# A hybrid mixer layer on one core: where the output weights are split, how many rooms the sample attention has, and in which round one product stands

## The chip, the cores and the metric

The kernel runs on one core of a Trainium2 chip. The metric is the device time of one execution in microseconds (us), the median of the runs. One more execution was taken by the profiler; all rows below come from it.

The engines are named as in the profile: PE (TensorE's matmuls; PEld its weight loads), DVE (VectorE), ACT (ScalarE), POOL (GpSimd) and SP (SyncE, which issues DMAs). SPq is SP's own queue.

## The reference, cut to what matters

One mixer layer is computed for a prompt of 1024 tokens and for 8 samples of 8 tokens (64 rows), 1088 rows in all, with the same weights. Three branches (retention, multi-scale pooling, sparse attention) are merged by sigmoid gates and go through one output projection.

```python
z = rms_norm(x, gain) @ w_in
o_a, s_ret_new = retention(rq, rk, rv, s_ret, pos0)          # 4 heads
b_a = (silu(rg) * o_a) @ w_br_a
o_b, pool_new = pool_mix(pu, pool_buf, pos0, w_pool, pool_scale)
b_b = (silu(pg) * o_b) @ w_br_b
o_c = nsa_attention(nq, kv_cmp, kv_sel, kv_win, ...)
b_c = (silu(ng) * o_c) @ w_br_c
merged = gates[0] * b_a + gates[1] * b_b + gates[2] * b_c
y = x + merged @ w_out                                        # w_out: 1024 x 1024
y = rms_norm(y, final_gain)
```

## The kernel before, in words

**Numbers in two halves.** A float32 operand is held as two float16 tiles, high and low part, and a product is three matmuls (high by high, low by high, high by low). `wsplit` (L220 to L224) makes the two parts of a weight: a scaled copy on ACT (L222), then a subtraction on DVE (L223).

**Stages.** `run` (L161) goes through the stages in order: keys and values of the prompt, prompt attention, retention (about 495 to 760 us of the profiled execution), the sample stage (760 to 887 us: the pooling branch and `sample_attention`), and `output` (from 887 us: the branch products and the merge by Strassen's scheme, and from 1212.6 us `out_rows`, the product with w_out).

**Retention.** 36 steps, 4 heads by 9 tiles of rows. Each step projects one tile (`proj_t`, 24 matmuls into a tile z) and moves the tiles in flight one stage on (`ret_tile`, a generator: rotation, rh, a transposing DMA qt, scores at and am, ah and al, output ro, state S and Sh). `load_r` fetches and splits the next head's weights (rwh, rwl) at the head's third tile. From the seventh step on, each step also calls the generator `sample_prep` once, which prepares the samples' compressed keys.

**Sample stage.** PE does the projections of the pooling branch (pj, L309 to L311, three matmuls of 384 or 320 columns per block) and between them `sample_attention`. That runs over four pairs of samples: keys and values into ks and vs, scores s, softmax in s and st (S and sums), transposes ta (L1089) and tb (L1091), their float16 parts sph (ACT, L1096) and spl (DVE, L1097), products so (L1108, L1111), their sum soc, and a transpose sto (L1117). The tiles svs, sks, sS and sst have one room each, so that a pair takes the room of the pair before it. Last in the stage's code, `out_weights` (L1504) fetches w_out in 8 blocks of 512 KB (tile wr), splits each (wh on ACT, wl on DVE, 128x1024) and stores both parts in DRAM (wod, two stores of 256 KB a block) for the output stage to read back.

**Output.** `out_rows` multiplies the merged rows (mm) by w_out in blocks of 128 rows by 512 columns; with Strassen's sums T1 to T4 of quarters of w_out, which are made beside it: DVE subtracts quarters (L1800) and `wsplit` splits the sums into tb, rm and T4a. A `prod` is 12 matmuls of 512 columns (L1841), a `plus` adds its result on DVE (L1846). The first round (four row blocks) does two products a block, then `remainder` does the last 64 rows, and the second round does five products a block: S2 by T2, S1 by T1, S4 by the plain quarter 22, S3 by T3, and 22 by T4. Behind them a block is finished: a square on ACT (L1849), a sum and a power (DVE L1854 and L416, POOL L417), and two multiplications on DVE (L1862, in the function `finish`), then the store. POOL adds the intermediate sums (L1915, L1922, L1925).

**What sets the order.** The code is recorded, and a scheduler then gives each engine one fixed list of instructions, by its own estimate of when each would be ready. A tile's number of rooms (`bufs`) and the pools bound how far it can interleave. Under `with self.behind()` the instructions are placed behind the marked ones of the main work. An engine takes its list in order.

## Time and profile before

| what | us |
|---|---|
| median of the runs | 1308.41 |
| the runs | 1307.53, 1308.41, 1314.39 |
| the profiled execution's own time | 1306.29 |
| its span | 1304.5 |
| PE busy in the span | 1251.3 (96%) |
| DVE busy | 912.2 (70%) |
| ACT busy | 631.3 (48%) |
| POOL busy | 525.2 (40%) |

The span is the time from the first to the last instruction that the profiler saw; the execution's own time is 1.8 us more, and the median of the runs another 2.1 us more. In the rows a matmul's duration contains its fill; the pitch of two matmuls is the difference of their starts. "Idle before" in square brackets is the time in which the engine had nothing to do just before an instruction, with what ended it.

### The profile page before, as it was taken

To read this page: it belongs to the slowest core of one execution; us is meant where nothing else is said; L and a number is where in the kernel's file an instruction comes from. 1 tells how busy PE (TensorE), PEld (TensorE's weight loads), DVE (VectorE), ACT (ScalarE), POOL (GpSimd) and SP (SyncE) were. 2 spreads that over 40 slices of the span, in tenths; PEclk is the share of its full clock that TensorE was granted. 3 is DMA by queue.
4 is the path that set the end of the run, shared out by engine and by line. 5 is a ranking of instruction groups with operands and counts; after the bars stand their busy time and mean duration, and the time that the engine had idled before them with its cause. 6 is when DMAs were issued, how large, how long until landed. Compare 5 with 4: busy or idle time off the path is not lost. (4 is left out here: it accounts for less than half of the span.)

```text
span 1304.5 us, 27795 instructions
## 1 busy us (share of the span) xinstructions
PE 1251.3 (96%) x10520; PEld 850.6 (65%) x10520; DVE 912.2 (70%) x2288; ACT 631.3 (48%) x1474; POOL 525.2 (40%) x561
## 2 busy tenths in 40 slices
PE   7999899989999989999999999999999999999997
PEld 4555566767677764555655565657788888888643
DVE  6648635788777864766766668663698877578975
ACT  5633436667676763555554454433544333213331
POOL 1122013567676751445553550101743566323133
PEclk9999899999999999999999999998999999999998
DMA  7766623698899996243741278327542211543632
GB/s 251 182 133 149 149 66 86 99 147 146 164 173 205 192 207 174 58 124 104 173 139 35 85 202 264 77 76 255 180 130 58 58 49 55 175 145 114 227 96 97
DMA packets 324315, 179.24 MB, mean 137 GB/s; under 512 B 204433, under 2 KB 298609, under 8 KB 323764
## 3 DMA queue, kind: packets, MB, share of 16 engines
q1 hardware_dynamic: 283844, 137.83, 45.3%
q10 hardware_dynamic: 35600, 26.32, 6.8%
q0 software_dynamic: 4736, 13.31, 3.2%
q8 instruction: 82, 1.34, 0.4%
q14 instruction: 53, 0.43, 0.1%
HBM read 98.80 MB, written 33.25 MB: 101 GB/s over the span
## 5 line engine op out<-in xcount | busy, mean ns | idle before, releaser
L761 POOL TENSOR_TENSOR hl<-S,hl 128x640 f16<-128x640 f32 (+7 forms) x128 | 153.8, 1210 | 142.5 <-DVE hl L760 96.6
L309 PE MATMUL pj<-xh,whi 128*128 128x384 f16 (+1 forms) x480 | 153.0, 319 | 2.4 <-ACT ue L1423 2.1
L310 PE MATMUL pj<-xl,whi 128*128 128x384 f16 (+1 forms) x480 | 153.0, 319 | 0.0
L311 PE MATMUL pj<-xh,wlo 128*128 128x384 f16 (+1 forms) x480 | 152.8, 318 | 0.0
L288 PE MATMUL z<-rwh,xh 128*128 128x512 f16 x256 | 97.0, 379 | 0.0
L290 PE MATMUL z<-rwh,xl 128*128 128x512 f16 x256 | 97.0, 379 | 0.0
L289 PE MATMUL z<-rwl,xh 128*128 128x512 f16 x256 | 97.0, 379 | 0.0
L756 ACT ACTIVATE S<-S,nm 128x640 f32<-128x640 f32 (+7 forms) x128 | 93.7, 732 | 5.2 <-DVE hst L852 0.9
L311 PEld LDWEIGHTS <-wlo 128*128 128x128 f16 x672 | 66.1, 98 | 36.6 <-issue 1.3
L310 PEld LDWEIGHTS <-whi 128*128 128x128 f16 x672 | 66.1, 98 | 36.1 <-issue 4.9
L1572 DVE TENSOR_TENSOR q<-st,q 128x288 f32<-128x288 f32 (+1 forms) x168 | 70.3, 433 | 26.4 <-PE st L1563 25.3
L309 PEld LDWEIGHTS <-whi 128*128 128x128 f16 x672 | 66.1, 98 | 33.6 <-issue 1.3
L288 PEld LDWEIGHTS <-xh 128*128 128x128 f16 x448 | 45.3, 101 | 46.4 <-issue 7.2
L290 PEld LDWEIGHTS <-xl 128*128 128x128 f16 x448 | 43.9, 98 | 44.9 <-issue 0.7
L222 ACT ACTIVATE whi<-raw 128x1024 f16<-128x1024 f32 (+1 forms) x48 | 45.5, 948 | 57.0 <-PE pj L310 14.7
L289 PEld LDWEIGHTS <-xh 128*128 128x128 f16 x448 | 43.9, 98 | 42.1 <-issue 0.9
L755 ACT ACTIVATE hl<-S,nm 128x128 f16<-128x128 f32 (+7 forms) x64 | 49.1, 767 | 36.6 <-DMA pt<-hl 36.5
L1328 PE MATMUL o<-vst,pt 128*128 128x64 f16 x528 | 56.3, 193 | 10.7 <-DMA pt<-hl 10.6
L760 DVE CAST hl<-S 128x640 f16<-128x640 f32 (+4 forms) x64 | 33.2, 519 | 45.9 <-ACT S L756 16.2
L1260 POOL TENSOR_TENSOR rh<-rot,rh 128x256 f16<-128x256 f32 (+1 forms) x36 | 26.5, 735 | 89.1 <-ACT rh L1259 88.9
L310 PE MATMUL eg<-xl,whi 128*128 128x384 f16 (+1 forms) x192 | 61.5, 320 | 0.0
L309 PE MATMUL eg<-xh,whi 128*128 128x384 f16 (+1 forms) x192 | 61.5, 320 | 0.0
(511 smaller groups left out, 4056.0 us busy)
## 6 DMA issues: line engine op xcount, KB each, us to landing
raw<-w_in SPq DMA_DIRECT2D x26, 512.0 KB
raw<-w_in ACTq DMA_DIRECT2D x18, 512.0 KB
raw<-w_in SPq DMA_DIRECT2D x48, 128.0 KB
wad<-q ACTq DMA_DIRECT2D x21, 256.0 KB
txd<-rso SPq DMA_DIRECT2D x8, 544.0 KB
raw<-egd SPq DMA_DIRECT2D x16, 272.0 KB
s<-state_ret SPq DMA_DIRECT2D x16, 256.0 KB
o_ret_s<-s POOLq DMA_DIRECT2D x16, 256.0 KB
```

The lines of the kernel that those rows point to most:

```text
L222: a = nc.scalar.activation(hi, raw, AF.Copy, scale=WS)
L288: nc.tensor.matmul(out, xh, hi[:, k, c0:c0 + n], start=(k == 0), stop=False)
L289: nc.tensor.matmul(out, xh, lo[:, k, c0:c0 + n], start=False, stop=False)
L290: self.marks["PE"] = nc.tensor.matmul(out, xl, hi[:, k, c0:c0 + n], start=False, stop=(k == 7))
L309: nc.tensor.matmul(out, hi[:, k, :], xh, start=(k == 0), stop=False)
L310: nc.tensor.matmul(out, hi[:, k, :], xl, start=False, stop=False)
L311: self.filled = nc.tensor.matmul(out, lo[:, k, :], xh, start=False, stop=(k == 7))
L755: nc.scalar.activation(hl[:, :w], s[:, d0:c1], AF.Exp, bias=nm[:, br:br + 1], scale=0.125)
L756: nc.scalar.activation(s[:, c0:c1], s[:, c0:c1], AF.Exp, bias=nm[:, br:br + 1], scale=0.125, accum_out=l[:, 0, br, r:r + 1])
L761: nc.gpsimd.tensor_tensor(hl[:, w:2 * w], s[:, d0:c1], hl[:, :w], op=ALU.subtract)
L1328: nc.tensor.matmul(out, lhs[0], rhs[0], start=start, stop=False)
L1572: nc.vector.tensor_tensor(out[:, c0:c0 + n], b, x[:, c0:c0 + n], op=ALU.add)
```

## The change

It has three parts.

- `out_weights` leaves the sample stage and becomes a generator that the retention steps once per tile from the seventh step on: one step fetches a block (and stores the block split before), the next splits it. Both tiles come from the pool `smc`, under the tag of the samples' raw rows, which has two rooms; a split block is stored by one DMA of 512 KB.
- The tiles svs, sks, sS and sst of `sample_attention` get two rooms each.
- In `out_rows` the product S4 by 22, with its `plus`, moves from the second round (behind the remainder) into the first (ahead of it). The number of products is the same.

```diff
@@ run
                 next(pool, None)
-                self.out_weights(self.pool(es, "wout"))
@@ sample rows
+    def sraw(self, pool):
+        return pool.tile([P, 2, 2, 256], F32, tag="sraw", name=self.nm("sraw"), bufs=2)
+
     def sample_rows(self, pool, b):
-        raw = pool.tile([P, 2, 2, 256], F32, tag="sraw", name=self.nm("sraw"), bufs=2)
+        raw = self.sraw(pool)
@@ sample_attention
-            vs = sp.tile([P, 2, 2, 2, 2, 2, 64], F16, tag="svs", name=self.nm("svs"))
-            ks = sp.tile([P, 2, 8, P], F16, tag="sks", name=self.nm("sks"))
+            vs = sp.tile([P, 2, 2, 2, 2, 2, 64], F16, tag="svs", name=self.nm("svs"), bufs=2)
+            ks = sp.tile([P, 2, 8, P], F16, tag="sks", name=self.nm("sks"), bufs=2)
...
-            s = sp.tile([P, 704], F32, tag="sS", name=self.nm("sS"))
-            st = sp.tile([P, 24], F32, tag="sst", name=self.nm("sst"))
+            s = sp.tile([P, 704], F32, tag="sS", name=self.nm("sS"), bufs=2)
+            st = sp.tile([P, 24], F32, tag="sst", name=self.nm("sst"), bufs=2)
@@ retention
-        prep = self.sample_prep(rp, psa)
+        prep, wout = self.sample_prep(rp, psa), self.out_weights()
...
             if n > 5:
                 with self.behind():
                     next(prep, None)
+                    next(wout, None)
@@ out_weights
-    def out_weights(self, pool):
+    def out_weights(self):
         self.wod = self.dr.tile([P, 8, 2, 1024], F16, name="wod")
-        for k in range(8):
-            raw = pool.tile([P, 1024], F32, tag="wr", name=self.nm("wr"), bufs=2)
+        hl = None
+        for k in range(9):
+            if hl is not None:
+                nc.sync.dma_start(self.wod[:, k - 1], hl.rearrange("p (a c) -> p a c", a=2))
+            if k == 8:
+                return
+            raw, out = [self.sraw(self.smc).rearrange("p a b c -> p (a b c)") for _ in range(2)]
             nc.sync.dma_start(raw, self.d["w_out"][0][k * P:(k + 1) * P, :])
-            hl = [pool.tile([P, 1024], F16, tag="w" + x, name=self.nm("w" + x), bufs=n) for x, n in (("h", 2), ("l", 1))]
-            self.wsplit(*hl, raw)
-            for a in range(2):
-                nc.sync.dma_start(self.wod[:, k, a], hl[a])
+            yield
+            hl = out.bitcast(F16)
+            self.wsplit(hl[:, :1024], hl[:, 1024:], raw)
+            yield
@@ out_rows
             plus(x[:, :512], prod("12", "21", c), x[:, :512])
+            plus(x[:, 512:], prod("S4", "22", c), x[:, 512:])
...
             plus(b0, p5, b0)
-            plus(b0, prod("S4", "22", c), b0)
```

How the lists of the engines stand at three places:

ACT in the retention, at one of the eight split steps. Line numbers of the changed kernel are a few off those of before: ga, vh, rh, Sh, ob are the casts of one tile's stages. Before:

```order
L1275 CAST ah_8368<-am_8366 128x128
L916 CAST ga<-to_1273_8400 128x2x2x32
L1250 ACTIVATE vh_8449<-z_8323 128x256
L1259 CAST rh_8453<-rot_8444 128x256
L1347 CAST Sh_8384<-S_8382 128x256
L1297 ACTIVATE ob_8389,rst_8388<-ro_8372 128x256
```

and now:

```order
L1278 CAST ah_8378<-am_8376 128x128
L915 CAST ga<-to_1277_8410 128x2x2x32
L221 ACTIVATE sraw_8331<-sraw_8330 128x1024
L1262 CAST rh_8465<-rot_8456 128x256
L1253 ACTIVATE vh_8461<-z_8333 128x256
L1350 CAST Sh_8394<-S_8392 128x256
L1300 ACTIVATE ob_8399,rst_8398<-ro_8382 128x256
```

The high part of a block of w_out (from sraw to sraw, 128x1024) now stands in ACT's list ahead of rh, vh and Sh of a tile.

PE at the last pair of samples, from the pooling product y to the first products so. Before:

```order
L311 MATMUL pj_12724<-xh,wlo_12655 128x320
L1467 MATMUL y_12752<-dd_12542,wpl 128x320
L1089 MATMUL ta_12039<-ident,sS_12016 128x128 x4
L1108 LDWEIGHTS sph_12047
L1108 MATMUL so_12055<-svs_11960,sph_12047 32x128
L1091 MATMUL tb_12044<-ident,sS_12016 128x128
L1092 MATMUL tb_12044<-ident,sS_12016 64x128
L1111 LDWEIGHTS spl_12048
```

and now:

```order
L309 MATMUL pj_12707<-xl,whi_12703 128x384
L1091 MATMUL ta_12088<-ident,sS_12065 128x128 x4
L310 LDWEIGHTS wlo_12704
L310 MATMUL pj_12707<-xh,wlo_12704 128x384
L308 LDWEIGHTS whi_12703
L308 MATMUL pj_12707<-xh,whi_12703 128x384
L309 LDWEIGHTS whi_12703
L309 MATMUL pj_12707<-xl,whi_12703 128x384
L310 LDWEIGHTS wlo_12704
L310 MATMUL pj_12707<-xh,wlo_12704 128x384
L1470 MATMUL y_12696<-dd_12377,wpl 128x320
```

Where so followed on ta at once, 19 projection matmuls and one y now stand between them; 9 more stand ahead of tb, and 22 and one y between the last so and sto, where none stood.

DVE in the second round of `out_rows`, around the third block's u3 (written from py and raw). Before:

```order
L1846 SCALAR_TENSOR_TENSOR xr<-py_17677,xr 128x512
L1846 SCALAR_TENSOR_TENSOR xr<-py_17691,xr 128x512
L1854 TENSOR_TENSOR yst_17192<-yst_17192 128x1
L416 TENSOR_SCALAR yst_17192<-yst_17192 128x1
L1862 SCALAR_TENSOR_TENSOR rm<-xr,yst_17192,rm 128x512 x2
L1846 SCALAR_TENSOR_TENSOR u_2686_17660<-py_17713,raw_17190 128x512
```

and now:

```order
L1855 SCALAR_TENSOR_TENSOR xr<-py_17685,xr 128x512
L1871 SCALAR_TENSOR_TENSOR rm<-rm,yst_17585 128x512 x2
L1863 TENSOR_TENSOR yst_17200<-yst_17200 128x1
L415 TENSOR_SCALAR yst_17200<-yst_17200 128x1
L1855 SCALAR_TENSOR_TENSOR u_2680_17668<-py_17707,raw_17198 128x512
L1871 SCALAR_TENSOR_TENSOR rm<-xr,yst_17200,rm 128x512 x2
```

One of two additions into xr is gone, the finish of the block before stands inside this block's chain, and u3 stands ahead of the block's own finish in this round (in the last round it still stands behind).

## Rows read from the trace of the kernel before

**Rows 1.** The page's first part: busy us, share of the span, instructions.

```profile
PE 1251.3 (96%) x10520; PEld 850.6 (65%) x10520; DVE 912.2 (70%) x2288; ACT 631.3 (48%) x1474; POOL 525.2 (40%) x561
```

**Rows 2.** Busy time by stretch: start and end, length, then PE, PEld, DVE, ACT and POOL busy us with instructions, granted clock, DMA share, GB/s. First the whole retention, then the sample stage and what follows.

```profile
495.00:760.00 265.00, 258.74 (x1706) 148.01 (x1705) 172.12 (x499) 134.96 (x395) 120.26 (x184) 1.00 0.41 108
...
790.00:810.00 20.00, 17.92 (x130) 11.32 (x128) 16.46 (x40) 11.62 (x26) 0.00 (x0) 1.00 0.76 247
810.00:870.00 60.00, 60.00 (x521) 37.41 (x520) 40.02 (x130) 23.24 (x59) 5.43 (x6) 1.00 0.34 80
...
880.00:890.00 10.00, 8.29 (x60) 5.32 (x60) 3.82 (x13) 1.78 (x5) 0.00 (x0) 0.56 0.95 355
890.00:900.00 10.00, 10.00 (x83) 7.70 (x82) 2.59 (x4) 4.25 (x11) 3.77 (x4) 0.93 0.60 191
```

**Rows 3.** What PE waited for between 760 and 895 us: line, releaser, us in total, times, longest.

```profile
PE pj L309 <- ACT ue L1423: 2.1, 1, 2.1
PE so L1108 <- ACT sph L1096: 1.5, 1, 1.5
PE tb L1091 <- DVE spl L1097: 1.2, 1, 1.2
PE sto L1117 <- DVE soc L1115: 0.7, 1, 0.7
PE so L1111 <- DVE spl L1099: 0.2, 1, 0.2
```

**Rows 4.** ACT's timeline around 798 us: start us, duration us, instruction, idle before it.

```profile
797.15 0.50 ACT L1472 CAST gb<-th 128x384 f16<-128x384 f32 x1
798.82 1.06 ACT L222 ACTIVATE wh<-wr 128x1024 f16<-128x1024 f32 x1 [1.17 <-DMA wr<-w_out]
799.79 0.47 ACT L1423 ACTIVATE ue<-pj 128x384 f32<-128x384 f32 x1
```

**Rows 5.** The instructions that touch the tile wr (ns min/median/max, first and last start).

```profile
L222 ACT ACTIVATE wh<-wr x8: 1057/1057/1058, 768.9 to 807.1; 128x1024 f16<-128x1024 f32 x8
L223 DVE SCALAR_TENSOR_TENSOR wl<-wr,wh x8: 1205/1221/1226, 771.4 to 808.4; 128x1024 f16<-128x1024 f32 x8
```

**Rows 6.** The longest of ACT's waits for a block of w_out, from the list of waits of ACT over the whole span (us in total, times, longest).

```profile
ACT wh L222 <- DMA wr<-w_out: 11.8, 6, 2.7
```

**Rows 7.** PE's timeline from the last pair's transposes to the branch products.

```profile
869.28 0.33 PE L309 MATMUL pj<-xh,whi 128*128 128x384 f16 x1
869.44 0.33 PE L310 MATMUL pj<-xl,whi 128*128 128x384 f16 x1
...
877.25 0.60 PE L1089 MATMUL ta<-ident,sS 128*128 128x128 f32 x4
879.32 0.23 PE L1108 MATMUL so<-svs,sph 128*32 128x128 f16 x1 [1.47 <-ACT sph L1096]
880.78 0.33 PE L1091 MATMUL tb<-ident,sS 128*128 128x128 f32 x1 [1.23 <-DVE spl L1097]
...
887.12 0.45 PE L1117 MATMUL sto<-ident,soc 128*128 128x128 f32 x1 [0.70 <-DVE soc L1115]
887.36 0.50 PE L1642 MATMUL pb<-gb,whi 128*128 128x352 f16 x1
887.65 0.50 PE L1643 MATMUL pb<-gb,whi 128*128 128x352 f16 x1
```

**Rows 8.** What PE waited for in the retention, 495 to 760 us.

```profile
PE ro L1328 <- ACT Sh L1347: 1.8, 1, 1.8
PE ro L1330 <- DVE al L1276: 1.5, 3, 0.7
...
PE ro L1328 <- ACT ah L1275: 1.0, 3, 0.4
```

**Rows 9.** The weight splits of the retention on ACT, 495 to 760 us, by form: count, busy us, mean ns, idle before them.

```profile
L222 ACT ACTIVATE rwh<-raw 128x512 f16<-128x512 f32 x27 | 16.6, 629 | 20.7 <-DMA raw<-w_in 20.7
...
L222 ACT ACTIVATE whi<-raw 128x1024 f16<-128x1024 f32 x4 | 4.2, 1057 | 3.0 <-DMA raw<-w_in 2.4 <-PE eg L310 0.7
```

**Rows 10.** The transposing DMAs that SP issues for the retention (ns min/median/max).

```profile
L1262 SPq DMA_TRANSPOSE qt<-rh x36: 1172/1194/2144, 506.3 to 748.0; - x36
```

**Rows 11.** PE's timeline from the end of the remainder in `out_rows`.

```profile
1240.52 0.38 PE L1841 MATMUL py<-tb,T 128*128 128x512 f16 x1 [0.31 <-ACT tb L222]
1242.81 0.93 PE L1841 MATMUL py<-tb,T 128*128 128x512 f16 x2 [1.91 <-DVE tb L223]
1243.53 3.71 PE L1841 MATMUL py<-tb,mm 128*128 128x512 f16 x10
1247.08 0.81 PE L1841 MATMUL py<-wo,T 128*128 128x512 f16 x3
...
1253.34 2.75 PE L1841 MATMUL py<-T4a,mm 128*128 128x512 f16 x12
1255.93 2.75 PE L1841 MATMUL py<-tb,T 128*128 128x512 f16 x12
```

**Rows 12.** DVE's timeline in the last two blocks of the second round.

```profile
1280.67 0.68 DVE L1846 SCALAR_TENSOR_TENSOR u<-py,raw 128x512 f32<-128x512 f32 x1
...
1292.35 1.41 DVE L1862 SCALAR_TENSOR_TENSOR rm<-xr,yst,rm 128x512 f32<-128x512 f32 x2 [0.73 <-POOL yst L417]
1293.68 0.68 DVE L1846 SCALAR_TENSOR_TENSOR u<-py,raw 128x512 f32<-128x512 f32 x1
```

## The prediction

> **What bounds the kernel now.** I read the page's first part first [rows 1]: PE is busy 1251.3 of 1304.5 us. What can be won is in the 53 us in which PE stands still or runs at a lower clock, so the next view is the busy time by stretch [rows 2]. In the retention (495 to 760 us) PE is busy 258.74 of 265. In the sample stage it loses 2.08 us between 790 and 810 and 1.7 us between 880 and 890, and there the granted clock drops to 0.56. The list of PE's waits for that stage [rows 3] names five, 2.1 + 1.5 + 1.2 + 0.7 + 0.2 = 5.7 us, and the timelines show how each comes about [rows 4, 7]. In the output stage PE waits twice, behind the remainder [rows 11]. These are the places that the change touches; elsewhere no product is added or taken away.
>
> **Part one, w_out leaves the sample stage.** At 800 us PE waits 2.1 us for ue [rows 3]. ACT was free after gb, at 797.15 + 0.50 = 797.65; it then stood 1.17 us in front of wh, whose block had not landed, took 1.06 us for the split, and only then did ue [rows 4]. Both the wait and the split leave the stage, 1.17 + 1.06 = 2.2 us, a little more than PE's wait: **-2.1 us**. The other seven splits cost PE nothing that the list shows, so nothing more is won from them here.
>
> **The same work in the retention.** Eight splits of 1.06 us on ACT and 1.22 us on DVE [rows 5] come into a stage whose PE is 97.6% busy [rows 2]. What a split does there can be read from those that stand there now: 27 of 0.629 us and 4 of 1.057 us on ACT [rows 9], 21.2 us, and with as many on DVE beside them PE waits for ACT's Sh and ah and DVE's al 1.8 + 1.0 + 1.5 = 4.3 us in the whole stage [rows 8]. That is 0.20 us of PE per us of split, so 8 x 1.06 = 8.5 us more give **+1.7 us**. The bounds: nothing, if the projections of the next tile cover every split (ACT is busy 135 of 265 us there [rows 2]); and if every split found its block as late as the worst in the sample stage, 8 x (2.7 + 1.06) = 30.1 us [rows 5, 6]. Below nothing it can't go, since work is only added here. I take 1.7, the row of the same work on the same engines in the same stage. Each of the eight steps also puts a fetch and a store on SP's queue among the transposes qt. A block is stored one step behind its split, 265 / 36 = 7.4 us, so the store should find it done, and SP's issue of one transpose, 1.19 us [rows 10], is the size of what a DMA holds up; I put that at nothing, covered by the 7.4 us that a step lasts. Without that cover it is 16 x 1.19 = 19 us on SP, spread over 36 steps.
>
> What stands in ACT's list behind a split waits for it: in rows 4, ue waits for wh, and PE for ue. The Trainium skill has the rule for it ("TensorE: Matmul & The Clock Gate", section "Architectural detail: the array is 16× 32×32, not 1× 128×128"): ACT's and DVE's queues are strictly first in, first out, and only PE pulls weight loads ahead. That speaks against this part, since the split now stands ahead of rh, vh and Sh; taken at its hardest, it is rival one below.
>
> **Part two, two rooms.** With one room, keys, values and scores of a pair had to wait for the pair before, and at the last pair PE had no projections left to put between the steps. In the row, so follows ta with 1.47 us idle, tb follows with 1.23, sto with 0.70 [rows 7], and 0.2 more for spl [rows 3]: 3.6 us. In the new order 19 projections and a y stand between ta and so, 9 projections ahead of tb, and 22 and a y ahead of sto. A projection's pitch is 869.44 - 869.28 = 0.16 us [rows 7], so the covers are over 3.0 us against 1.47, 1.4 against 1.23, and 3.5 against 0.70. The first and the last are ample, the middle one is thin; I leave half of its 1.23 standing: **-3.0 us**. The bounds are 0 (the waits come back elsewhere in the stage) and -3.6.
>
> **The clock behind those waits.** From 880 to 890 us the granted clock is 0.56, from 890 to 900 0.93 [rows 2]. The pitch of a matmul of 352 columns there is 887.65 - 887.36 = 0.29 us, where one of 384 columns took 0.16 before [rows 7], so PE ran at 1.2 GHz instead of 2.4. What it did before the fall: it ran at full clock until two idle pieces of 1.47 and 1.23 us came within 3 us, with only a few small products between them. Between 810 and 870 us, where the products of the other pairs stand among projections, PE was busy 60.00 of 60 and the clock 1.00 [rows 2]. With the last pair's products now among projections too, I expect that state there. The price is 0.44 x 8.29 + 0.07 x 10.00 = **-4.35 us**, with the bounds 0 and -4.35.
>
> **Part three, S4 in the first round.** Behind the remainder PE waits 0.31 and 1.91 us for split sums of w_out, tb [rows 11]. Then 12 matmuls go at 0.355 us (from 1243.53 to 1247.08 for ten) instead of 2.59 / 12 = 0.216: 1.7 us more. Four products of 2.59 us now stand ahead of the remainder, 10.4 us for DVE to finish the sums in, so both should go: 3.9 us. But the second round loses cover. Before, five products of 2.59 us made 12.95 us a block, and u3 of the last two blocks stand 1293.68 - 1280.67 = 13.0 us apart [rows 12]. Now four make 10.4. In that interval DVE, POOL and ACT form one chain in turn, of which only one `plus` of 0.69 us goes. If it keeps its length, 12.3 us, the end follows the chain: the round starts 10.4 - 3.9 = 6.5 us later, its first u3 comes a product (2.6) sooner, and three intervals are 0.7 us shorter: 6.5 - 2.6 - 2.1 = +1.8 us. If PE sets the pace, it is 6.5 - 2.6 - 3 x 2.59 = -3.9. The new order lets the blocks overlap (a finish stands inside the next block's chain), and DVE's own work in a block is 5 x 0.69 + 2 x 1.41 = 6.3 of 10.4 us, so PE's pace is nearer; for the last block, where u3 still stands behind the finish, I leave a third: **-2.6 us**.
>
> **The sum.** -2.1 + 1.7 - 3.0 - 4.35 - 2.6 = -10.35 us against the profiled execution's own 1306.29, so 1295.9. The median of the runs shown is 2.1 above that execution: 1308.41 - 10.35 = **1298.1 us**.
>
> **The rivals.**
>
> *One, ACT in the retention gives most of it back.* Each split delays rh, vh or Sh by its full 1.06 us and PE with it: 8 x 1.06 = 8.5 instead of 1.7, so 1298.1 + 6.8 = 1304.9. For it: Sh already held PE 1.8 us once [rows 8]. Against: ACT waits 20.7 us there for weights to split [rows 9], and only 4.3 us of PE's waiting comes of all of it.
>
> *Two, the sample chain stays.* Two rooms move the four pairs together, DVE and ACT become late at some other pair, and the clock falls there: 3.0 + 4.35 are not won, 1305.4. For it: the thin cover ahead of tb. Against: DVE was busy 40.0 of 60 us between 810 and 870 [rows 2], and gets rid of the splits.
>
> *Three, the second round is bound by its chain*: +1.8 in place of -2.6, 1302.5. For it: u3 comes behind the finish of its own block in the last interval [rows 12]. Against: the order as told above.
>
> *Four, slower: ACT stands in front of blocks of w_out that have not landed.* The place is the eight split steps of the retention; the price 3.76 us each as bounded above, 30.1 in place of 1.7: 1298.1 + 28.4 = 1326.5. The other terms win 12.05 us, so the kernel is slower than before from 12.05 / 8 = 1.5 us of PE's time a split on, and by over 0.5% (6.5 us) from 2.3. For it: ACT did wait for w_out before six splits of eight [rows 6]. Against: the DMA share was 0.76 there and is 0.41 here [rows 2], and a block is asked for a whole step of 7.4 us ahead. SP is another way to the same end, if a store should wait at its head while qt stands behind it. The Trainium skill ("DMA: Bandwidth & Descriptors", section "Anatomy of one DMA — SWDGE (gpsimd) path") says that a DMA's wait happens on the sequencer that issues it, before dispatch; by it each split that is late holds the transposes too. No row here shows a store in that place.
>
> **How the numbers follow.** The chances: the forecast 0.64, rival one 0.11, two 0.08, three 0.10, four 0.07. The forecast's own range is 1294.5 (all gains in full, the splits free: -2.1 - 3.6 - 4.35 - 3.9 = -13.95) to 1301.8. A change under 0.5%, some 6.5 us, a measurement of this kernel can hardly tell from none; so faster means below 1301.9 and slower above 1314.9. Faster: the forecast and over half of rival three, 0.70. Same: rivals one and two and the rest of three, 0.23. Slower: rival four, 0.07. The range that should hold the time 8 times in 10 reaches from 1293.5, a us below the full gains, to 1305.5, past rivals one to three.
>
> **What would show it.** Around 800 us no wait of PE for ue. At the last pair so, tb and sto without idle time, and no stretch of the sample stage and the first branch products at a granted clock below 0.95. In the retention PE waits for ah, al and Sh 5 to 8 us in all instead of 4.3; over 10 says rival one, and ACT waiting for sraw from w_out says rival four. Behind the remainder no wait for tb and full clock; the u3 of the second round 10.4 to 11 us apart, or over 12, which is rival three. The prediction is wrong if the loss in the retention exceeds some 8 us, or if the low clock shows up at another place of the sample stage.

## The result, and the profile after

The change made the kernel slower: 1320.76 us (median of 8 runs, 1316.79 to 1323.14) against 1309.78 (8 runs, 1307.44 to 1314.39), ratio 1.0087, 95% interval 1.0069 to 1.0106: slower by under 1%, but clear of the noise. The forecast, 1298.1, is on the wrong side, and 1320.76 lies above its range. The profiled execution took 1321.18 us, its span is 1319.4, 14.9 more than before. One run in the whole document, of all3_tx below, took 1447.65 us at a granted clock of 0.848 where the kernel's others had 0.985 to 0.989; it is left out of that kernel's ratio.

PE's line of the page after, against [rows 1]: PE is busy 6.1 us longer with the same 10520 products, so part of the loss is clock or spacing of matmuls, the rest standing still.

```profile
PE 1257.4 (95%) x10520; PEld 852.1 (65%) x10520; DVE 919.5 (70%) x2288; ACT 631.1 (48%) x1474; POOL 527.6 (40%) x561
```

To see where, I cut both spans at products that both kernels have. The first and last start of ro<-vh,ah bound the retention, those of pb<-gb the first products of the pooling branch. The lines of these products (ns min/median/max, first and last start), before:

```profile
L1328 PE MATMUL ro<-vh,ah x32: 272/273/283, 519.8 to 755.0; 128*128 128x256 f16 x32
```

and after:

```profile
L1331 PE MATMUL ro<-vh,ah x32: 272/273/283, 522.6 to 764.2; 128*128 128x256 f16 x32
L1651 PE MATMUL pb<-gb,whi x128: 242/278/313, 892.8 to 945.0; 128*128 128x352 f16 x64, 128*128 128x192 f16 x64
```

The stages' lengths in us, cut the same way in every profile (the rounds end with the last start of py<-T4a):

| kernel | ahead | retention | sample stage | pooling products | merge | output rounds | tail |
|---|---|---|---|---|---|---|---|
| before | 519.8 | 235.2 | 132.4 | 46.2 | 279.0 | 82.1 | 9.8 |
| after | 522.6 | 241.6 | 128.6 | 52.2 | 280.2 | 77.9 | 16.3 |
| difference | +2.8 | +6.4 | -3.8 | +6.0 | +1.2 | -4.2 | +6.5 |

The instructions ahead of the retention are the same in both kernels; over all kernels here that part took 519.6 to 524.3 us (519.8 to 524.2 in those that leave the retention alone), so its +2.8 can't be put down to the change.

Busy time by stretch, columns as in [rows 2], first before:

```profile
519.80:755.00 235.20, 230.22 (x1553) 133.41 (x1553) 157.51 (x471) 123.56 (x368) 113.39 (x175) 1.00 0.39 102
755.00:887.40 132.40, 126.68 (x1008) 80.42 (x1007) 92.68 (x249) 57.14 (x134) 23.00 (x23) 0.98 0.58 169
```

then after: the retention, five us each around its worst place, the sample stage, the pooling products, and last the place where the clock was low before and a place of the sample stage where it is low now:

```profile
522.60:764.20 241.60, 234.72 (x1554) 134.86 (x1554) 167.98 (x478) 130.93 (x376) 115.32 (x175) 0.98 0.47 134
...
585.00:590.00 5.00, 1.47 (x22) 0.97 (x16) 3.67 (x8) 2.17 (x6) 2.68 (x3) 1.00 0.73 222
590.00:595.00 5.00, 4.10 (x19) 2.57 (x18) 3.86 (x16) 3.75 (x12) 3.77 (x6) 0.51 0.48 148
595.00:600.00 5.00, 5.00 (x21) 2.03 (x20) 4.96 (x6) 4.38 (x13) 2.91 (x3) 0.81 0.14 43
...
764.20:892.80 128.60, 126.43 (x1006) 79.60 (x1005) 81.89 (x238) 47.84 (x125) 22.57 (x23) 0.99 0.33 82
892.80:945.00 52.20, 45.88 (x384) 34.45 (x382) 26.73 (x33) 23.93 (x54) 18.15 (x13) 1.00 0.72 238
...
870.00:900.00 30.00, 28.70 (x216) 19.10 (x215) 17.93 (x45) 12.05 (x31) 0.00 (x0) 1.00 0.36 111
...
810.00:815.00 5.00, 4.51 (x31) 2.25 (x28) 4.05 (x12) 1.98 (x6) 0.00 (x0) 0.69 0.64 157
```

The last row but one shows that the half clock of [rows 2] is gone from its place, as forecast; the last one, that the clock is now low earlier in the sample stage, 0.69 from 810 to 815 us. That is a sign which the prediction had named for being wrong. The 6.3 us in which PE stands among the pooling products, and the low clock in the retention, are new too.

**The retention: one late block.** PE's waits there, first after and against [rows 8]; then those of the sample stage, against [rows 3], and the longest of the pooling products:

```profile
PE ro L1331 <- ACT ah L1278: 5.3, 3, 3.5
PE ro L1333 <- DVE al L1279: 1.5, 3, 0.9
...
PE so L1110 <- ACT sph L1098: 0.9, 1, 0.9
PE tb L1093 <- DVE spl L1099: 0.5, 1, 0.5
...
PE pb L1651 <- ACT mm L1707: 5.0, 7, 1.1
```

The wait of 3.5 us for ah can be followed back through the timelines of SP, ACT and PE (start, duration, instruction, idle before it), in order of time:

```profile
553.56 3.00 SPq L968 DMA_DIRECT2D sbr<-btab  x8
556.68 1.94 SPq L1357 DMA_DIRECT2D s<-state_ret  x4
...
559.18 0.43 SPq L1519 DMA_DIRECT2D sraw<-w_out  x1
559.98 9.90 SPq L1265 DMA_TRANSPOSE qt<-rh  x2
...
565.82 1.06 ACT L221 ACTIVATE sraw<-sraw 128x1024 f16<-128x1024 f32 x1 [2.14 <-DMA sraw<-w_out]
566.78 0.39 ACT L1262 CAST rh<-rot 128x256 f16<-128x256 f32 x1
...
569.98 0.53 SPq L1515 DMA_DIRECT2D wod<-sraw  x1
570.60 0.38 SPq L1519 DMA_DIRECT2D sraw<-w_out  x1
571.03 0.78 SPq L273 DMA_DIRECT2D raw<-w_in  x1
...
588.08 0.63 ACT L221 ACTIVATE rwh<-raw 128x512 f16<-128x512 f32 x1 [2.59 <-DMA raw<-w_in]
...
589.28 0.28 ACT L1278 CAST ah<-am 128x128 f16<-128x128 f32 x1
...
589.62 0.28 PE L1331 MATMUL ro<-vh,ah 128*128 128x256 f16 x1 [3.53 <-ACT ah L1278]
...
591.02 0.39 PE L1333 MATMUL ro<-vh,al 128*128 128x256 f16 x1 [0.90 <-DVE al L1279]
```

The fetch of a block stands on SP behind twelve other loads. It went out at 559.18, 4.5 us before ACT came to the split (565.82 - 2.14 = 563.68), and its block was there 6.6 us after the issue. Behind the split stood rh, from which SP's next transpose qt is made (the second of the two that fill 9.90 us of SP's queue); behind that transpose SP had a store and a fetch of w_out, and only then the next head's weights (raw<-w_in). The first of these went out 48.4 us behind the retention's first product (571.03 - 522.6); before, it was 43.7 us (563.48 - 519.8). One of the later ones was 2.59 us late for ACT at 588.08, and ah stood behind its split. Then PE had two idle pieces, 3.53 and 0.90 us, and the granted clock of the next 5 us was 0.51, of the 5 after that 0.81.

**The pooling products: loads in another order.** SP and ACT after, around the start of that stage:

```profile
895.76 1.40 SPq L1674 DMA_DIRECT2D T<-txd  x3
896.42 1.08 ACTq L1492 DMA_DIRECT2D T4a<-w_br_a  x2
...
909.94 1.15 ACT L221 ACTIVATE q<-T4a 128x512 f16<-128x512 f32 x2 [10.20 <-DMA T4a<-w_br_a]
```

and before:

```profile
881.25 1.29 SPq L1665 DMA_DIRECT2D T<-txd  x3
...
888.44 1.02 ACTq L1489 DMA_DIRECT2D T4a<-w_br_a  x2
...
894.15 1.15 ACT L222 ACTIVATE q<-T4a 128x512 f16<-128x512 f32 x2 [1.53 <-DMA T4a<-w_br_a]
```

Before, the three loads of txd (1088 KB each) went out 7.2 us ahead of the first loads of w_br_a; after, 0.7 us. ACT got w_br_a 909.94 - 896.42 = 13.5 us after the issue instead of 5.7 and stood 10.2 us in front of it; what ACT copies out of PSUM for PE (mm) stood behind that, and PE waited 5.0 us for it.

**The output.** DVE after, against [rows 12], with a wait for a quarter of w_out in the first line and the end of the remainder in the next two:

```profile
1241.31 0.69 DVE L1809 TENSOR_TENSOR q<-q,q 128x512 f32<-128x512 f32 x1 [1.78 <-DMA q<-w_out]
...
1267.39 0.68 DVE L1896 TENSOR_TENSOR rm<-rm 64x512 f32<-64x512 f32 x1 [2.21 <-ACT rm L319]
1269.88 2.46 DVE L1871 SCALAR_TENSOR_TENSOR rm<-rm,yst 64x512 f32<-64x512 f32 x2
...
1276.34 0.68 DVE L1855 SCALAR_TENSOR_TENSOR u<-py,raw 128x512 f32<-128x512 f32 x1
...
1285.06 0.68 DVE L1855 SCALAR_TENSOR_TENSOR u<-py,raw 128x512 f32<-128x512 f32 x1
...
1294.65 0.68 DVE L1855 SCALAR_TENSOR_TENSOR u<-py,raw 128x512 f32<-128x512 f32 x1
1295.40 2.43 DVE L1871 SCALAR_TENSOR_TENSOR rm<-xr,yst,rm 128x512 f32<-128x512 f32 x2
...
1308.56 0.69 DVE L1855 SCALAR_TENSOR_TENSOR u<-py,raw 128x512 f32<-128x512 f32 x1
```

PE no longer waits anywhere in the output ([rows 11] had 1.91 and 0.31 us). But the span ends 10.8 us behind the last u3 in both kernels (1319.4 - 1308.56 and 1304.5 - 1293.68), and after, PE's product for the first u3 ended well before it was used:

```profile
1266.94 2.75 PE L1850 MATMUL py<-rm,T 128*128 128x512 f16 x12
```

1266.94 + 2.75 = 1269.69, and u3 follows at 1276.34, 6.65 us later. Before, DVE stood ready and waited for that product:

```profile
1253.54 0.69 DVE L1846 SCALAR_TENSOR_TENSOR u<-py,raw 128x512 f32<-128x512 f32 x1 [0.82 <-PE py L1841]
```

### The profile page after: what moved, and what is told of

It is laid out like the page before. It is cut to its first block, busy times and chain, and to the rows that moved or that the text cites. A ratio compares the mean times of both kernels' runs of the same rounds, so it can differ in the third digit from the quotient of the medians.

```text
span 1319.4 us, 27777 instructions
## 1 busy us (share of the span) xinstructions
PE 1257.4 (95%) x10520; PEld 852.1 (65%) x10520; DVE 919.5 (70%) x2288; ACT 631.1 (48%) x1474; POOL 527.6 (40%) x561
## 5 line engine op out<-in xcount | busy, mean ns | idle before, releaser
L310 PE MATMUL eg<-xh,wlo 128*128 128x384 f16 (+1 forms) x192 | 61.4, 320 | 0.0
```

What stands on the lines that cost most here:

```text
L310: self.filled = nc.tensor.matmul(out, lo[:, k, :], xh, start=False, stop=(k == 7))
```

## The experiments

Fifteen kernels. Each has its median, then the ratio of its runs to those of the kernel before that ran with it, and the ratio's 95% interval; the ratio is not exactly the quotient of the two medians. What a part does alone comes first. Part two was run only on top of part one, so what the second rooms do to the kernel before is not known.

**a_only** is the changed kernel without parts two and three (**ab**: without part three alone):

```diff
-            vs = sp.tile([P, 2, 2, 2, 2, 2, 64], F16, tag="svs", name=self.nm("svs"), bufs=2)
+            vs = sp.tile([P, 2, 2, 2, 2, 2, 64], F16, tag="svs", name=self.nm("svs"))
...
-            plus(x[:, 512:], prod("S4", "22", c), x[:, 512:])
...
             plus(b0, p5, b0)
+            plus(b0, prod("S4", "22", c), b0)
```

> The kernel before with part one alone (w_out split in the retention; one room for the sample tiles, S4 in the second round). Theory 'late weights', from the trace of the changed kernel: the fetches and stores of w_out in the retention make the next head's weights land later, ACT stands in a split waiting for them (26 us in all instead of 21), ah and Sh behind it come late, PE waits 1.5 to 3.5 us at a time and the granted clock falls behind the wait: +6 in the retention, -2 at 800 us where PE waited for ue, so 1312 to 1316 where the kernel before has 1309.8. Rival 'as forecast' (splits cost their own share only, 1.7): no change to -0.5, 1309 to 1310.

> The changed kernel with S4 back in the second round (parts one and two). Theory 'displaced loads': two rooms take the waits out of the last pair (-5) but put the last projections, and with them the loads of the input sums txd, later; these collide with the loads of w_br_a, ACT waits some 10 us for those, and the branch products lose 7: so 2 to 5 us slower than part one alone, 1316 to 1320, and 1 to 4 us faster than the changed kernel, since the second round keeps its cover. Rival 'rooms win': 5 to 8 us faster than part one alone.

Measured: a_only 1315.28 us, 1.0048 (1.0031 to 1.0065); ab 1317.79, 1.0067 (1.0041 to 1.0094). So part one loses by itself, as expected; that the rooms add to the loss (0.19%) is not clear of the noise here. Stages of a_only: retention 243.6, sample stage 124.4, pooling products 52.2, the output (rounds and tail) 90.2; of ab 240.2, 128.5, 51.3, 90.3. The sample stage of a_only:

```profile
764.00:888.00 124.00, 124.00 (x1005) 78.65 (x1003) 82.16 (x237) 47.78 (x124) 20.86 (x23) 1.00 0.38 93
```

PE is busy throughout at full clock with one room. What I had credited to part two, part one does. Whether by the other order of that stage or by the work and transfers that left it (169 GB/s before, 93 here), no run separates. With the second rooms there are waits again, and in ab a low clock, at another pair:

```profile
808.00:824.00 16.00, 16.00 (x134) 9.79 (x133) 9.21 (x38) 6.70 (x20) 0.00 (x0) 0.90 0.20 40
```

**c_only** moves S4's product alone, **c_first** moves it for the first block only (the edit shown):

```diff
             plus(x[:, :512], prod("12", "21", c), x[:, :512])
+            if i == 0:
+                plus(x[:, 512:], prod("S4", "22", c), x[:, 512:])
...
-            plus(b0, prod("S4", "22", c), b0)
+            if i:
+                plus(b0, prod("S4", "22", c), b0)
```

> The kernel before with part three alone. Theory 'chain': the stall of 3.9 us behind the remainder goes, but with four products a block the second round follows the chain of DVE, POOL and ACT, so +1 to +3, 1311 to 1313; PE ends over 12 us ahead of the end instead of 9.5. Rival, as forecast: -2.6, 1307; PE ends 9.5 to 11 us ahead.

> The kernel before with S4 by 22 of the first row block alone moved into the first round (the other three stay in the second). One product of 2.59 us covers the 2.2 us of waiting behind the remainder, and three of four blocks keep five products of PE work a block. Theory 'chain': the gain of 2 to 4 us comes through to the end, 1306 to 1308. Rival 'the finish of the remainder and the first block bind anyway': no change, 1309 to 1310.5.

Measured: c_only 1310.07, 1.0016 (0.9996 to 1.0036); c_first 1308.30, 0.9996 (0.9976 to 1.0015). The output took 91.9 us in both, as in the kernel before. The loss of 1 to 3 us expected of c_only can't be told from nothing, and the gain expected of c_first did not come. In c_first, PE still waits 1.9 us for tb.

In c_only no wait of PE is left in the output, and nothing is won all the same: u3 starts at 1265.46, 1274.17, 1283.73 and 1297.64, 8.7, 9.6 and 13.9 us apart, as in the kernel after.

**dma_add and split_add** take the retention's new work apart, on the kernel before, which keeps its own splits in the sample stage. The first adds the eight fetches and stores at their places and no split (nobody reads what is stored), the second eight splits of a tile that is always there, and no transfer:

```diff
...
+        for k in range(9):
+            if k:
+                nc.sync.dma_start(dst[:, k - 1], raw)
+            if k == 8:
+                return
+            raw = self.sraw(self.smc).rearrange("p a b c -> p (a b c)")
+            nc.sync.dma_start(raw, self.d["w_out"][0][k * P:(k + 1) * P, :])
+            yield
+            yield
```

```diff
...
+        for k in range(8):
+            yield
+            self.wsplit(hl[:, :1024], hl[:, 1024:], raw)
+            yield
```

> The kernel before, unchanged in its three places, with transfers added in the retention at the changed kernel's steps: eight fetches of 512 KB of w_out and eight stores of 512 KB into an unused piece of DRAM, without any split. Theory 'late weights': the transfers make the next head's weights late, ACT's waits for them grow from 21 to 25 us or more, PE waits for ah and Sh, +4 to +7: 1313 to 1316. Rival 'occupied ACT' (the splits' own time and place do the damage): no change, 1308 to 1310.

> The kernel before with eight splits of 128x1024 added on ACT and DVE in the retention at the changed kernel's steps, of a tile that lies in SBUF all the time, without any transfer. Theory 'late weights': the splits cost only their share, 0 to +2: 1309 to 1311. Rival 'occupied ACT': the greater part of part one's loss, +4 to +7: 1313 to 1316.

Measured: 1309.39, 0.9992 (0.9974 to 1.0011), and 1308.89, 0.9994 (0.9974 to 1.0015); retention 236.3 and 236.8 us against 235.2. Alone, the transfers cost 1.1 and the splits 1.6 us there, little more than the kernels with an unchanged retention differ by (234.3 to 235.2). So the loss that was expected of the transfers did not come, and the 6.4 need both. What the traces show only in kernels with both is a split in the retention that waits for its transfer.

**a_late** makes part one's splits late in the retention (from step 25 on, one block a step), so that split, fetch and store come together. The edit against a_only, without the generator's new order:

```diff
-                    next(wout, None)
+                    if n >= 25:
+                        next(wout, None)
```

> Part one alone, but w_out is fetched and split from the 26th step on (one block a step), when the last head's weights are in. Theory 'late weights': the retention's loss of 5 to 8 us goes, the loss behind it stays: 1309 to 1311. Rival: splits anywhere in the retention cost the same, 1314 to 1317.

Measured: 1320.80, 1.0091 (1.0057 to 1.0124), retention 245.6 us; the expectation, 1309 to 1311, failed. ACT now waits for rooms still being stored:

```profile
ACT sraw L221 <- DMA wod<-sraw: 16.5, 6, 4.6
```

So late in the retention, too, much waiting of ACT in front of w_out goes with a long retention; which of the new waits makes it was not followed.

**a_tx and ab_tx** take a_only and ab and put the first two loads of w_br_a on SP, ahead of the three of txd:

```diff
-            for i, x in ((2, "T2"), (1, "T3"), (3, "T4")):
-                nc.sync.dma_start(tx[x], self.txd[:, i])
...
+                                    nc.sync if p == pairs[0] else None)
+                if p == pairs[0]:
+                    with self.tc.issue_after(self.loaded.ins):
+                        for i, y in ((2, "T2"), (1, "T3"), (3, "T4")):
+                            nc.sync.dma_start(tx[y], self.txd[:, i])
```

> Part one alone (1315.3 in its run), with the first two loads of w_br_a on SP's queue ahead of the three loads of the input sums txd instead of on ACT's queue beside them. Theory 'displaced loads': the 10 us in which ACT waits for w_br_a go to 3 us or less, PE's waits for mm behind the pooling products go, -5 to -7 against part one alone: 1308 to 1310. Rival: the sums txd are then late themselves or ACT waits as long: within 2 us of part one alone.

> Parts one and two, with w_br_a ahead of the sums txd. Against part one with the same edit (1309.1) it tells what the second rooms do by themselves. Theory 'rooms lose': with two rooms the scheduler lets the first pairs come closer together, PE waits for sph, spl and os near the second pair and the clock falls there, +2 to +4: 1311 to 1313. Rival 'rooms are neutral': 1308.5 to 1310.

Measured: a_tx 1309.08, 1.0007 (0.9983 to 1.0031), ab_tx 1315.22, 1.0035 (1.0018 to 1.0052): 0.4% and 0.3% below a_only and ab (the intervals of the first pair meet, those of the second overlap). ab_tx was expected lower, at 1311 to 1313. The pooling products take 47.8 and 48.2 us instead of 52.2 and 51.3. The timeline of a_tx:

```profile
889.68 1.44 SPq L1492 DMA_DIRECT2D T4a<-w_br_a  x2
891.49 2.41 SPq L1705 DMA_DIRECT2D T<-txd  x3
...
894.90 1.15 ACT L221 ACTIVATE q<-T4a 128x512 f16<-128x512 f32 x2 [2.48 <-DMA T4a<-w_br_a]
```

The same bytes in the other order end ACT's wait of 10.2 us (10.5 in a_only). The edit also moves the two loads from ACT's queue to SP's; the order alone was not run. Between the two kernels only the rooms differ; they cost 0.28% by the ratios, with intervals that overlap a little.

**a_txq** asks whether SP's transposes among the weight loads hold these up. The second qt of a head goes behind its last weight load:

```diff
-        self.marks["SP"] = nc.sync.dma_start_transpose(qt[:, :, :m], rh[:m].rearrange("p a c -> p (a c)"))
+        self.nq = getattr(self, "nq", 99) + 1
+        with ExitStack() as eq:
+            if self.nq == 2:
+                eq.enter_context(self.tc.issue_after(self.rload.ins))
+            self.marks["SP"] = nc.sync.dma_start_transpose(qt[:, :, :m], rh[:m].rearrange("p a c -> p (a c)"))
```

> Part one with w_br_a ahead of the sums txd (1309.1 in its run), and in SP's list the second transpose qt behind a head's weight loads placed behind the last of these loads, as it stood in the kernel before; nothing else is moved. Theory 'qt ahead of loads': in the changed kernel's list a qt, which waits for POOL's rh, stands ahead of the last two to four weight loads of a head; these go out late, ACT waits in the split for them, and ah comes 3.5 us late; with the order of before the retention's 5 to 8 us go, 1303 to 1306. Rival (the fetches, stores and splits of w_out themselves make the loss): within 2 us of 1309.

Measured: 1315.16, 1.0037 (1.0020 to 1.0054), retention 245.0 us, sample stage 129.6; expected were 1303 to 1306. Between the first and the last ro<-vh,ah ACT waits for weights as long as before the edit (14.2 us, 13.8 in a_tx), and PE now stands in front of qt:

```profile
PE at L1336 <- DMA qt<-rh: 4.5, 2, 3.5
```

That reason falls: the loads are as late behind the first transpose alone (567.73, first load 570.07).

**pool_sub and a_txq_ps** try to win DVE's time in the output, by T3's and T4's subtractions on POOL, on the kernel before and on a_txq:

```diff
-                nc.vector.tensor_tensor(b[o], b[x], b[y], op=ALU.subtract)
+                (nc.gpsimd if t in ("T3", "T4") else nc.vector).tensor_tensor(b[o], b[x], b[y], op=ALU.subtract)
```

> The kernel before with eight of the sixteen subtractions of w_out's quarters in the output product (those of T3 and T4) on POOL instead of DVE. Theory 'DVE sets the end': moving S4 gained nothing because DVE, busy without a gap from 1215 to 1248 us, sets the pace of the whole stage and not PE's wait; 8 x 0.6 = 4.8 us less on DVE bring the end 2 to 4 us nearer, 1305.5 to 1307.5. Rival: the chain of the second round sets the end alone, or POOL is slower than what it relieves: 1308.5 to 1311.

> All that helped together: part one, w_br_a ahead of txd, qt behind the weight loads, and the subtractions of T3 and T4 on POOL; one room, S4 in the second round. If the gains add up, 1300 to 1304; if the subtractions on POOL bring nothing, as a_txq.

Measured: 1317.29, 1.0056 (1.0036 to 1.0076), and 1323.09, 1.0092 (1.0071 to 1.0113); the output takes 99.2 and 99.0 us instead of 91.9 and 92.3. Both expected gains failed. In pool_sub POOL and DVE run beside each other:

```profile
1226.59 1.26 POOL L1800 TENSOR_TENSOR q<-q,q 128x512 f32<-128x512 f32 x1 [6.86 <-ACT tb L222]
1226.61 1.80 DVE L223 SCALAR_TENSOR_TENSOR tb<-q,tb 128x512 f16<-128x512 f32 x1
```

POOL takes 1.26 us for what DVE does in 0.69, and DVE's split beside it 1.80 instead of 0.69.

**a3, a3_tx and all3_tx** give each block of w_out three steps instead of two, one more between fetch and split: on a_only, on a_tx, and on the whole change with the loads as in a_tx:

```diff
             nc.sync.dma_start(raw, self.d["w_out"][0][k * P:(k + 1) * P, :])
             yield
+            yield
             hl = out.bitcast(F16)
```

> Part one with three steps a block, w_br_a where the changed kernel has it. Theory 'one split that waits' with 'displaced loads': the retention's loss is gone, the loss behind the sample stage stays (pooling products 51 to 53 us instead of 46), 1309 to 1312. Rival 'added work': as part one alone, 1314 to 1317.

> Part one with w_br_a ahead of the sums txd, and with one more step between a block's fetch and its split in the retention (three steps a block instead of two). Theory 'one split that waits': in all kernels with part one ACT waits 1.6 to 3.0 us for one block of w_out that has not landed, rh stands behind it, then qt on SP, then the next head's weight loads behind qt, and 20 us later ah is 3.5 us late and the clock falls; with a further step the block has landed: ACT waits for no block, the retention takes 235 to 238 us instead of 241, 1303 to 1306 in all. Rival 'added work in the retention': fetches, stores and splits together make the loss wherever the split stands: 240 us or more, 1308 to 1310.

> The whole change (split in the retention, two rooms, S4 in the first round) with both repairs: three steps a block, and w_br_a ahead of txd. If the two mechanisms are what the change lost by, the second rooms and S4 cost 2 to 4 and 0 to 2 more than the same kernel without them: 1307 to 1311, level with the kernel before. Rival (the losses have other causes): 1314 or more.

Measured: a3 1312.27, 1.0017 (1.0000 to 1.0033); a3_tx 1306.37, 0.9972 (0.9954 to 0.9989); all3_tx 1312.67, 1.0006 (0.9987 to 1.0025). The first two lie just above what was expected, the third 1.7 us. In all three ACT waits for no block of w_out, and in a3_tx its waits for weights between the first and the last ro<-vh,ah are 7.1 us, where the kernel before has 8.3 and a_tx 13.8:

```profile
ACT rwh L221 <- DMA raw<-w_in: 7.1, 9, 1.5
```

The retention is 235.8 us in a3_tx (a_tx 241.0) and 234.2 in all3_tx, but 238.9 in a3, where PE waits 2.40 us for al and 2.00 us for ah at other places. In a_only, ab, a_tx, ab_tx, a_txq and after, with two steps a block, one wait of 1.6 to 3.0 us for a block stands in each, and a wait of PE of 3.4 to 3.8 us comes 23 to 24 us behind it (for ah, in a_txq for qt). Of the kernels without the first, none but a_late has a wait of PE over 2.7 us in the retention. a3_tx beats both kernels; the whole change with the same two repairs does not beat the kernel before. Between these two lie the rooms and S4, 0.34% by the ratios; in the profiles 2.5 us in the sample stage and 94.5 - 90.2 = 4.3 in the output.

How much of the 4.3 us is S4's hangs on the clock behind the remainder, which differs between kernels with the same code there. PE's wait of 1.9 to 2.1 us for tb stands in every kernel with all of S4 in the second round and the subtractions on DVE. In six of these eleven the half clock of [rows 11] follows it (before, dma_add, split_add, a_tx, ab_tx, a_txq), and the output takes 91.7 to 93.6 us. In the other five (a_only, ab, a_late, a3, a3_tx) the clock stays at 1.00 and the output takes 90.2 to 90.4. In a_only, for one, behind waits of 0.38 and 1.93 us:

```profile
1251.35 2.32 PE L1850 MATMUL py<-tb,mm 128*128 128x512 f16 x10
```

These are the ten products that took 3.71 us before. So all3_tx's 94.5 us are 4.1 to 4.3 above the kernels at full clock, but only 0.9 to 2.8 above those with the low clock.

## Why the prediction was wrong

The sum was -10.35 us; the profiled spans differ by +14.9. The gap of 25.3 is: sample stage and pooling products together -9.45 forecast (the wait for ue, the last pair, the clock) and -3.8 + 6.0 = +2.2 found, 11.7 us off; retention +1.7 and +6.4, 4.7 off; output -2.6 and -4.2 + 6.5 = +2.3, 4.9 off; the merge, 1.2 longer, not predicted and not explained (279.8 to 280.5 us in most kernels with part one, 278.7 to 279.5 in those without); and 2.8 in the part that did not change.

**Part one in the sample stage: right, and more.** The wait for ue is gone, as forecast (-2.1). What I had not read is that the waits of the last pair would go with w_out's splits too: with one room for keys and scores the stage took 124.4 us in a_only, 8.0 less than before. It is not always so short with one room: in a3, a_txq_ps and a_txq PE waits 1.3 to 2.0 us there for the keys (sks), and the stage takes 126.0 to 129.6.

**The retention: the cover of 7.4 us failed.** The prediction put a block's transfer under "a whole step" and SP's queue at nothing. In the rows a fetch stood behind twelve loads on SP; 4.5 us were left, and it took 6.6. That is rival four's mechanism at one block of eight, and SP's transposes handed it on to the next head's weights. The term of work was about right: the splits alone cost 1.6 us where 1.7 was forecast, though that is little more than unchanged retentions differ by. Rival four's price was not: its 30.1 us counted each block as late, and one was. 6.4 / 8 = 0.8 us a split is below the 1.5 from which it was to turn the sign. The loss also stays under the 8 us that I named as the sign of a wrong prediction (in a_only it is 8.4), and PE's waits for ah and al, 5.3 + 1.5 = 6.8 us, lie in the 5 to 8 that I named for the forecast; but ACT's wait for sraw, the sign of rival four, is there. The sign turned since other gains failed too. Part of the price is clock, which the forecast didn't count in this stage: 0.49 x 4.10 + 0.19 x 5.00 = 3.0 us in the ten us behind the wait. That a waiting split holds rh back agrees with the Trainium skill's rule that I weighed ("TensorE: Matmul & The Clock Gate", section "Architectural detail: the array is 16× 32×32, not 1× 128×128"): ACT's queue is first in, first out. The trace agrees, rh standing at 566.78 behind the split of 565.82. I had priced the rule with 1.06 us a split, and it acted through the wait. That the wait was handed on through qt to the weights is read from the traces, and a_tx against a3_tx fits it; no run stops the chain at one link alone.

That an earlier fetch mends it is shown as far as the three kernels with a third step go: none has the wait for a block or PE's long wait behind it, and the retention takes 235.8, 234.2 and, with waits elsewhere, 238.9 us. The third step also moves the splits to other places, so it is not shown that the longer lead alone does it; split_add, where the splits stood at the old places and cost 1.6, speaks for the lead.

**The pooling products: no term at all.** The prediction had products of PE and splits of ACT in view, and took the first branch products as the place where the clock recovers. That the loads behind the sample stage would be issued later, and so closer together, was on no line of it. In a_only SP issues the raw<-w_in ahead of txd's loads at 890.37, 2.3 us behind the stage's first product, in the kernel before at 879.75, 7.7 us ahead of it. That the loads' order or queue makes the greater part of the loss is shown by a_tx and ab_tx, where these products took 1.6 and 2.0 us longer than before, instead of 6.0 and 5.1; why SP comes to that load later, I only argue: projections now run to the end of the stage and free the weights' last room late.

**Part two: credited with part one's gain.** -3.0 for the last pair and -4.35 for the clock did arrive in the main (with the wait for ue 8.0 of 9.45 us), but in a_only, with one room. The step that failed is that one room made the pair wait. With two rooms the clock fell elsewhere, 0.69 from 810 to 815 us. That the rooms themselves cost is likely, not shown: 0.19% between a_only and ab, 0.28% between a_tx and ab_tx, each small against its intervals; the sample stage is longer in all three pairs of profiles (128.5 against 124.4, 132.0 against 124.5, 127.4 in all3_tx against 124.9 in a3_tx), but a_txq, with one room, has 129.6. In the profiles with two rooms it is rival two, the late pair elsewhere, and its "thin cover ahead of tb" still has 0.5 us of waiting. Two things had gone together in the order of before and now that I read, and I gave both to the one that was nearer.

**Part three: rival three, by the end if not by its sum.** It gave +1.8, found are +2.3 (in c_only's profile 0.0). PE's waits went. The distances of u3 are 8.7, 9.6 and 13.9 us: their mean, 10.7, is the 10.4 to 11 of the forecast, and the last one is the "over 12" of the rival. The step that failed is "its first u3 comes a product sooner". Counted from the output's first product, it was to come 6.5 - 2.6 = 3.9 us later than before. It came 10.2 us later (1276.34 - 1225.2 = 51.1 against 1253.54 - 1212.6 = 40.9), and 6.65 us behind the end of its product; before, it started within 0.1 us of that end (1251.83 + 1.67 = 1253.50). DVE waits 2.21 us there for ACT, then its two finishes take 2.46 us, and only then the first block's chain begins. The chain of DVE, POOL and ACT never catches up: last u3 7.8 us behind its product (1298.02 + 2.75 = 1300.77). That PE's stall behind the remainder had covered the remainder's own end fits this; no run tests it alone.

Two more things bear on this part. DVE's wait of 1.78 us for a quarter of w_out is in the kernel after and, with 1.2 us, in all3_tx, whose output takes 94.2 and 94.5 us (c_first has one of 1.5); in c_only DVE waits 0.2 us in all for w_out, the same u3 starts 49.0 us behind the first product, and the output takes 91.9. Why the quarter was late is open. And the 1.7 us for the clock were booked as if each wait for tb cost them: five kernels of eleven had the wait without the low clock.

## What to carry to other kernels

Work that is moved brings its loads, and the place of a load in its queue decides: count the loads ahead of it there and its lead in us, and see what stands behind the instruction that would wait for it, through every queue that the wait is handed on to. A stall that a change removes may be cover for another engine; before it is booked, look whether the chain that ends the stage is PE's, and whether the low clock behind the stall is there in other profiles too. And where two parts of a change move the same order, no gain belongs to either until one has been run without the other.

## What the runs showed of the hardware

- One wait of PE of 3.53 us, with 0.90 more 1.4 us later, was followed by a granted clock of 0.51 for 5 us and 0.81 for the next 5. It cost some 3 us on top of the wait. A wait of 1.9 us in the output was followed by half the clock in six kernels and by full clock in five, with the same code in that stage; so one profile does not tell which clock will follow such a wait.
- DVE slows down beside POOL. The finish's pairs of 128x512, 1.41 us [rows 12], took 2.43 and 2.50 while POOL added tiles of the same size. POOL took 1.81 beside the first (below) and 1.27 beside the second, 1.26 in pool_sub's row. The Trainium skill ("GPSIMD Engine Reference", section "Specifications") has the two engines share their interfaces to SBUF, with contention where a DVE instruction has two inputs there; these have, and the rows agree. A `plus`, which reads one of its inputs from PSUM, took its usual 0.69 us at 1278.40 with POOL busy beside it.

```profile
1295.47 1.81 POOL L1931 TENSOR_TENSOR rm<-rm,u 128x512 f32<-128x512 f32 x1
```

- Two loads of w_br_a landed 5.7 us after their issue where txd's three loads had gone out 7.2 us earlier, and 13.5 us after it where both went out within 0.7 us, though from two queues. That agrees with the Trainium skill ("DMA: Bandwidth & Descriptors", section "Issuing engines are not separate DMA queues"): transfers started by different engines run on the same DMA engines and interleave.
- The 520 us ahead of the retention, with the same instructions, took 519.6 to 524.3 us over the profiled executions: a term of two us can't be read from one pair of profiles' spans.
